# Four-head decoder layer on one Trainium2 core: the third head's scores and value products as split float32r products, like the last head's

## The chip, the core and the metric

The kernel runs on one core of a Trainium2 chip. The metric is the time of one launch on the device in microseconds (us); lower is better. The engines in the text are TensorE (PE in the profile, its weight loads PEld), VectorE (DVE), ScalarE (ACT), GpSimd (POOL) and the queues that issue transfers: SP's own and ACT's (ACTq), which issues them in the order of ACT's instructions.

## The reference

One layer over 512 positions of width 1024: conditioned RMS norm, one input projection, four matrix-memory heads (mLSTM) of width 256 beside a gated convolution group, an output projection, and a gated feed-forward part with a short convolution. All is float32. The part that matters here is a head. The reference does it by chunks:

```python
scores = jnp.einsum("bhtd,bhsd->bhts", q_, k_) * jnp.exp(dmat - m_t[..., None])
num = (w_inter[..., None] * jnp.einsum("bhtd,bhde->bhte", q_, C)
       + jnp.einsum("bhts,bhse->bhte", scores, v_))
den = w_inter * jnp.einsum("bhtd,bhd->bht", q_, n) + jnp.sum(scores, axis=-1)
h = num / jnp.maximum(jnp.abs(den), jnp.exp(-m_t))[..., None]
```

The kernel has no chunks with a carried state: it forms the whole causal 512 x 512 matrix of weighted scores of a head, in four block rows of keys, and multiplies it by the values with a column of ones, which gives numerator and denominator together.

## The kernel before

**Two kinds of product.** A float32 matmul is issued to PE as two instructions. For nearly all large products the kernel does something else: it splits each operand into a rounded part hi (float32r, made by an ACT copy) and the rest lo (source less hi, made by a subtraction on DVE or POOL), and adds up hi·hi, hi·lo and lo·hi as three float32r matmuls (`mm3`, lines 186 to 190). `w_split` (164) splits weights with ACT and POOL, `pair` (451) splits an activation with ACT and DVE.

**The heads.** For head h, `head_load` (475) brings the weights of q, k and the output gate as three pieces of 1 MB (`wqko`), and `head_proj(h, i)` (481) makes the six projections of 128 x 512: i = 0, 1 for q, 2, 3 for k, 4, 5 for the gate `so`. A q or k goes through `conv4` (456): one ACT instruction at line 460, three taps on DVE at line 462, a silu on ACT at 463. `make_v(h)` (416) makes the values in four blocks, `make_E(h)` (598) the four block rows of decay factors E.

**attention(h)** (500) is a generator, so that its pieces can be put between the projections of the next head. First come the scores, one PSUM tile `s` per block row cc (keys cc·128 on, 512, 384, 256 and 128 columns), two at a time; DVE multiplies each into E (line 515). Then the products with the values, one tile `o` for each block tt of positions (1, 2, 3 and 4 block products, ten in all); ACT reads each `o` (lines 536 to 538). After that DVE scales (549), PE transposes into two tiles `hT` (555), and DVE and ACT make the head's result in two parts (557 to 561).

**Which head is split.** `SPLIT = (H - 1,)` (412) names the heads whose scores and value products are done by three float32r products instead of float32 matmuls. In the kernel before that is head 3 alone.

**Order.** PE and SP run in the order of the code. DVE, ACT and POOL get theirs from a scheduler at build time, which puts the 31-tap convolution (`cv_block`, 714, line 731 on DVE) and the conditioning sums (`ada_block`, 147: a load on the ACT queue into one of two buffers, then a product with a sum on DVE at line 155, tile `junk`) behind all else. Every engine then runs its list strictly in order. In the loop at 782, with h = 2, PE does: scores 0 and 1 of head 2, projection 0 of head 3, scores 2 and 3, projections 1 and 2, `o` 0 and 1, projection 3, `o` 2, projection 4, `o` 3, projection 5, then the values of head 3 with the two `hT` in between.

**Buffers.** PSUM is shared out as four banks for projections and values (`mmbank`, 87) and two (`atbank`, 90) that `s`, `o`, `hT` and a few others take in turn: a new one can begin when the tile two before it has been read. In SBUF there are 44 slots of 128 x 512 for q, k, E, their parts and the rest.

Of the kernel before, what the change touches and what calls it, by code (L numbers as in the profile page):

```python
# [22 lines left out]
H = 4  # L23
# [29 lines left out]
def decoder_layer(ctx, tc, w_glu0, x, xT, c, adaT, vecs, w_glu, w_qko, w_v0, w_v, w_out, w_up, w_down, out):  # L53
# [30 lines left out]
    def slot(name, dt=F32):  # L84
        return slots.tile([P, T], dt, tag="t", name=name)
# [78 lines left out]
    def w_split(src, name, pool=None, tag="w", eng=None):  # L164

        n = src.shape[1]
        pool = pool or wpool
        hi = pool.tile([P, T], F32R, tag=tag, name=f"{name}h")
        lo = pool.tile([P, T], F32R, tag=tag, name=f"{name}l")
        S.activation(hi[:, :n], src, AF.Copy)  # L170
        (eng or G).tensor_tensor(out=lo[:, :n], in0=src, in1=hi[:, :n].bitcast(F32), op=ALU.subtract)  # L171
        return hi, lo
# [236 lines left out]


    vs = [None] * H
    SPLIT = (H - 1,)
    gz = const.tile([P, NT, 2 * H], F32, name="gz")
    GB = 2 * H

    def make_v(h):
# [3 lines left out]
        for q in range(0, KT, 4):  # L420
# [6 lines left out]
            else:  # L427
                wv += [tuple(w[:, :n] for w in w_split(r[:, i * n : (i + 1) * n], f"wv{h}_{q + i}")) for i in range(4)]
        dt = F32R if h in SPLIT else F32
        va = vpool.tile([P, 2 * T + 8], dt, tag="vh", name=f"v{h}").rearrange("p (c n) -> p c n", c=NT)  # L430

        V.tensor_copy(va[:, :, DH:], ones[:, None, :2].to_broadcast([P, NT, 2]))
        vs[h] = [va[:, cc, :] for cc in range(NT)]
        if h in SPLIT:
            vl = [slot(f"vl{h}_{i}", F32R) for i in range(2)]
# [3 lines left out]
        for tt, ps in enumerate(banks):  # L439
# [5 lines left out]
            S.activation(va[:, tt, :DH], ps[:, :DH], AF.Copy)  # L445
            if h in SPLIT:
                V.tensor_tensor(out=vl[tt], in0=ps[:, :DH], in1=va[:, tt, :DH].bitcast(F32), op=ALU.subtract)
# [52 lines left out]
    def attention(h):  # L500

        _, qs, ks, so = heads[h]
        two = h in SPLIT
        if two:
# [277 lines left out]
    for h in range(H - 1):  # L782
# [14 lines left out]
        next(steps)  # L797
        if h + 1 in SPLIT:
            for zs in heads[h + 1][1:3]:
# [538 lines left out]
```

## Time and profile before

| | |
|---|---|
| median of 3 runs | 771.67 us (771.31 to 774.28) |
| the profiled execution: its time, its span | 773.07 us, 771.4 us |
| granted TensorE clock, mean | 0.997 |
| busy in the span: PE, DVE, ACT, POOL | 758.4, 610.1, 403.8, 352.2 us |
| scores of head 2 in the span | 261.3 to 264.5 and 269.9 to 272.0 us |
| value products of head 2 | in three groups from 282.9, 289.6 and 296.4 us |
| scores of head 3 | 317.9 to 320.4 and 323.2 to 324.5 us |

How to read the profile: a row of the timeline gives the start in us from the begin of the span, the duration of the row, engine, line, operation, tile written and tiles read, shapes, the count of merged instructions, and in brackets the idle time of the engine just before with what released it. Matmuls are pipelined, so a row's duration overlaps the next row; what a matmul costs PE is the distance from its start to the next start. DVE rows overlap the next by some 0.08 us in the same way.

### The profile page before, as it was taken

The numbers are of one execution on the slowest core, as the hardware profiler recorded it, in microseconds if no ns is written. First come the engines' busy times: TensorE is split into PE (matmuls) and PEld (weight loads), VectorE is DVE, ScalarE is ACT, GpSimd is POOL, SyncE is SP. The second block draws the span as 40 slices with busy tenths as digits, with TensorE's granted clock in tenths as the row PEclk, the third lists the DMA queues.
The fourth block names the chain that finished last, engine by engine and source line by source line (L and its number), as shares of the span: only waits on it lengthen the run. The fifth ranks groups of instructions, "written<-read, shape, count | busy, mean of one in ns | idle before, by whom it ended". The sixth has DMA issues, their size and how long they took to land.

```text
span 771.4 us, 10631 instructions
## 1 busy us (share of the span) xinstructions
PE 758.4 (98%) x3709; PEld 637.5 (83%) x3709; DVE 610.1 (79%) x967; ACT 403.8 (52%) x761; POOL 352.2 (46%) x286
## 2 busy tenths in 40 slices
PE   7999999999999999999999999999999999999996
PEld 5788898778888888988888998888888888888885
DVE  6997999999999966756768798666556687799995
ACT  5447266776666447582253555444444444455762
POOL 2029578696798645443661456444444440000001
PEclk9999999999999999999999999999999999999998
DMA  8983214214022452434953753332233321777872
GB/s 320 377 301 132 90 55 164 82 40 151 30 84 107 153 179 105 164 110 164 366 199 126 253 197 130 130 130 88 110 117 129 130 89 62 255 271 241 298 260 109
DMA packets 36409, 125.33 MB, mean 162 GB/s; under 512 B 4194, under 2 KB 5634, under 8 KB 30468
## 3 DMA queue, kind: packets, MB, share of 16 engines
q1 hardware_dynamic: 24372, 96.17, 35.5%
q10 hardware_dynamic: 11984, 28.48, 10.6%
q8 instruction: 29, 0.48, 0.3%
q14 instruction: 24, 0.20, 0.1%
HBM read 113.22 MB, written 11.42 MB: 162 GB/s over the span
## 4 chain that ended last, share of the span: by engine, by line
PE 72%; DVE 21%; DMA 2%; ACT 2%; issue 2%; POOL 0%; ACTq 0%; DVEq 0%; POOLq 0%
PE up L189 10%; PE up L188 10%; DVE cv L731 10%; PE up L190 10%; PE p L1185 4%; PE glu L189 3%; PE glu L190 3%; PE glu L188 3%; PE p L189 3%; PE p L188 3%; PE p L190 3%; PE mixa L188 2%; PE mixa L190 2%; PE mixa L189 2%; PE mixb L189 2%; PE mixb L188 2%
## 5 line engine op out<-in xcount | busy, mean ns | idle before, releaser
L731 DVE SCALAR_TENSOR_TENSOR cv<-gt,cvw,cv 128x505 f32<-128x505 f32 (+24 forms) x200 | 137.3, 729 | 2.3 <-ACT cv L719 1.1
L685 POOL TENSOR_TENSOR ro2r<-ro2t,mhalf 128x1 f32<-128x1 f32 x1 | 0.5, 537 | 119.8 <-DVE ro2t L683 119.8
L727 POOL TENSOR_TENSOR cs<-cs,cs 128x510 f32<-128x510 f32 (+3 forms) x32 | 41.9, 1308 | 0.3
L171 POOL TENSOR_TENSOR wup_1024l<-wup,wup_1024h 128x512 fp32r<-128x512 f32 x20 | 27.4, 1372 | 31.6 <-ACT wup_1024h L170 31.6
L171 POOL TENSOR_TENSOR wup_0l<-wup,wup_0h 128x512 fp32r<-128x512 f32 x20 | 27.7, 1387 | 30.0 <-ACT wup_0h L170 30.0
L171 POOL TENSOR_TENSOR wup_1536l<-wup,wup_1536h 128x512 fp32r<-128x512 f32 x20 | 28.0, 1399 | 27.6 <-ACT wup_1536h L170 25.1
L155 DVE SCALAR_TENSOR_TENSOR junk<-ada,cb 128x1024 bf16<-128x1024 f32 x20 | 31.3, 1565 | 8.5 <-DMA ada<-in_adaT 8.4
L189 PE MATMUL up<-u2l,wup_0h 128*128 128x512 f32 (+1 forms) x100 | 36.5, 365 | 0.2 <-DVE u2l L910 0.2
L188 PE MATMUL up<-u2h,wup_0h 128*128 128x512 f32 (+1 forms) x100 | 36.5, 365 | 0.0
L188 PE MATMUL up<-u2h,wup_1024h 128*128 128x512 f32 (+1 forms) x100 | 36.4, 364 | 0.0
L190 PE MATMUL up<-u2h,wup_0l 128*128 128x512 f32 (+1 forms) x100 | 36.4, 364 | 0.0
L188 PE MATMUL up<-u2h,wup_512h 128*128 128x512 f32 (+1 forms) x100 | 36.4, 364 | 0.0
L189 PE MATMUL up<-u2l,wup_512h 128*128 128x512 f32 (+1 forms) x100 | 36.4, 364 | 0.0
L190 PE MATMUL up<-u2h,wup_512l 128*128 128x512 f32 (+1 forms) x100 | 36.4, 364 | 0.0
L188 PE MATMUL up<-u2h,wup_1536h 128*128 128x512 f32 (+1 forms) x100 | 36.4, 364 | 0.0
L189 PE MATMUL up<-u2l,wup_1536h 128*128 128x512 f32 (+1 forms) x100 | 36.4, 364 | 0.0
L190 PE MATMUL up<-u2h,wup_1536l 128*128 128x512 f32 (+1 forms) x100 | 36.4, 364 | 0.0
L190 PE MATMUL up<-u2h,wup_1024l 128*128 128x512 f32 (+1 forms) x100 | 36.4, 364 | 0.0
L189 PE MATMUL up<-u2l,wup_1024h 128*128 128x512 f32 (+1 forms) x100 | 36.3, 363 | 0.0
L171 POOL TENSOR_TENSOR wup_512l<-wup,wup_512h 128x512 fp32r<-128x512 f32 x20 | 27.7, 1383 | 14.0 <-ACT wup_512h L170 14.0
L725 ACT ACTIVATE cs<-gt,cvw 128x511 f32<-128x511 f32 (+4 forms) x40 | 27.4, 716 | 6.5 <-POOL cs L727 3.2
L170 ACT ACTIVATE wup_1024h<-wup 128x512 fp32r<-128x512 f32 x22 | 13.9, 631 | 25.1 <-PE up L189 20.4
(1072 smaller groups left out, 2667.0 us busy)
## 6 DMA issues: line engine op xcount, KB each, us to landing
wup<-in_w_up SPq DMA_DIRECT2D x22, 1024.0 KB, 6.5
wqko<-in_w_qko SPq DMA_DIRECT2D x12, 1024.0 KB, 4.8
ada<-in_adaT ACTq DMA_DIRECT2D x20, 512.0 KB, 4.6
ada<-in_adaT SPq DMA_DIRECT2D x16, 512.0 KB, 6.9
wo<-in_w_out SPq DMA_DIRECT2D x8, 1024.0 KB, 4.8
spare<-in_adaT ACTq DMA_DIRECT2D x12, 512.0 KB, 7.4
wd<-in_w_down SPq DMA_DIRECT2D x6, 768.0 KB, 6.7
g2kept<-g2d SPq DMA_DIRECT2D x11, 384.0 KB, 7.3
```

The lines of the kernel that those rows point to most:

```text
L155: t = V.scalar_tensor_tensor(out=junk, in0=r, scalar=1.0, in1=cb, op0=ALU.mult, op1=ALU.mult, accum_out=mod[:, i : i + 1])
L170: S.activation(hi[:, :n], src, AF.Copy)
L171: (eng or G).tensor_tensor(out=lo[:, :n], in0=src, in1=hi[:, :n].bitcast(F32), op=ALU.subtract)
L188: PE.matmul(ps, a[0], b[0], start=start, stop=False)
L189: PE.matmul(ps, a[0], b[1], start=False, stop=False)
L190: PE.matmul(ps, a[1], b[0], start=False, stop=stop)
L685: G.tensor_tensor(out=r, in0=t, in1=mhalf[:, :1], op=ALU.pow)
L725: S.activation(t[:, d:], cvx[j][:, : T - d], AF.Copy, scale=w(CK - 1 - d))
L727: G.tensor_tensor(out=side[:, d:], in0=side[:, d:], in1=t[:, d:], op=ALU.add)
L731: last_tap[0] = V.scalar_tensor_tensor(out=cp[:, d:], in0=cvx[j][:, : T - d], scalar=w(CK - 1 - d), in1=cp[:, d:], op0=ALU.mult, op1=ALU.add)
L1185: PE.matmul(ps[q], x, y, start=False, stop=m == NM - 1 and i == 2, skip_group_check=True)
```

## The change

Head 2 joins the heads that are split:

```diff
-    SPLIT = (H - 1,)
+    SPLIT = (H - 2, H - 1)
```

This one line selects branches that are there already. In `make_v(2)` the values are stored as a float32r part, still by one ACT copy per block, and line 447 adds a subtraction on DVE for the rest (`vl`), which reads the PSUM bank of the block too. In the loop, after projection 4 of head 2, its two q and two k tiles are split by `pair`. In `attention(2)`:

```python
if two:
    mm3(sp[:, :n], [z[:, cc * P : (cc + 1) * P] for z in ks[d]], [z[:, cc * P :] for z in qs[d]], d == 0, d == 1)
else:
    PE.matmul(sp[:, :n], ks[d][:, cc * P : (cc + 1) * P], qs[d][:, cc * P :], start=d == 0, stop=d == 1)
...
if two:
    E[h][cc] = pair(E[h][cc], *halves_e[cc])
...
    PE.matmul(o[:, : DH + 2], eh, vh, start=cc == 0, stop=False)
    PE.matmul(o[:, :DH], eh, vl, start=False, stop=False)
    PE.matmul(o[:, : DH + 2], el, vh, start=False, stop=cc == tt)
else:
    PE.matmul(o[:, : DH + 2], E[h][cc][:, a : a + P], vs[h][cc], start=cc == 0, stop=cc == tt)
```

So PE has 3 instructions for every 2 in head 2's scores and value products. DVE gets 12 instructions more: four `qkl`, four `vl`, four `El`. ACT gets 8 more: four `qkh`, four `Eh`. No transfer is added, and outside head 2 nothing is computed in another way. The order on DVE and ACT is made anew.

On DVE, the four `qkl` of head 2 come between the taps of the last convolution block (tile `cv`, columns 492 downward); `dm` belongs to head 1:

```order
 L731 SCALAR_TENSOR_TENSOR cv_2298<-gt_912,cvw,cv_2298 128x492
+L453 TENSOR_TENSOR qkl_2480<-q_0c,qkh_2479 128x512
 L731 SCALAR_TENSOR_TENSOR cv_2298<-gt_912,cvw,cv_2298 128x491
-L432 CAST v_3021<-ones 128x4x2
+L432 CAST v_3093<-ones 128x4x2
+L453 TENSOR_TENSOR qkl_2484<-q_1c,qkh_2483 128x512
 L543 TENSOR_TENSOR dm_2379<-dm_2379,em 128x4
 L731 SCALAR_TENSOR_TENSOR cv_2298<-gt_912,cvw,cv_2298 128x490
+L453 TENSOR_TENSOR qkl_2488<-k_2c,qkh_2487 128x512
+L453 TENSOR_TENSOR qkl_2492<-k_3c,qkh_2491 128x512
 L731 SCALAR_TENSOR_TENSOR cv_2298<-gt_912,cvw,cv_2298 128x489
```

All that follows on DVE (the rest of the taps, then the conditioning sums and the E of head 2) stands behind them; the four `vl` are put in one by one further down, the last of them just ahead of the first E.

On DVE, from the first E of head 2 to the taps of head 3's first q (`q_0c`). Before:

```order
L515 SCALAR_TENSOR_TENSOR E_2510<-s_0_2720,E_2510 128x512
L155 SCALAR_TENSOR_TENSOR junk_3180,mod<-ada_3178,cb 128x1024
L515 SCALAR_TENSOR_TENSOR E_2511<-s_1_2724,E_2511 128x384
L155 SCALAR_TENSOR_TENSOR junk_3184,mod<-ada_3182,cb 128x1024
L155 SCALAR_TENSOR_TENSOR junk_3188,mod<-ada_3186,cb 128x1024
L160 TENSOR_TENSOR mod<-mod,vec 128x8
L667 SCALAR_TENSOR_TENSOR gains<-mod,vec 128x8
L515 SCALAR_TENSOR_TENSOR E_2512<-s_2_2759,E_2512 128x256
L462 SCALAR_TENSOR_TENSOR q_0c<-qko_0_2728,vec,q_0c 128x511
L515 SCALAR_TENSOR_TENSOR E_2511<-s_3_2763,E_2511 128x128
L462 SCALAR_TENSOR_TENSOR q_0c<-qko_0_2728,vec,q_0c 128x510
L462 SCALAR_TENSOR_TENSOR q_0c<-qko_0_2728,vec,q_0c 128x509
```

And with the change, from the third row of that stretch (E 0 and E 1 now stand together just ahead of it) to the second tap:

```order
L155 SCALAR_TENSOR_TENSOR junk_3248,mod<-ada_3246,cb 128x1024
L453 TENSOR_TENSOR El_2745<-E_2526,Eh_2742 128x512
L155 SCALAR_TENSOR_TENSOR junk_3252,mod<-ada_3250,cb 128x1024
L453 TENSOR_TENSOR El_2746<-E_2527,Eh_2743 128x384
L515 SCALAR_TENSOR_TENSOR E_2528<-s_2_2799,E_2528 128x256
L155 SCALAR_TENSOR_TENSOR junk_3256,mod<-ada_3254,cb 128x1024
L515 SCALAR_TENSOR_TENSOR E_2527<-s_3_2809,E_2527 128x128
L462 SCALAR_TENSOR_TENSOR q_0c<-qko_0_2768,vec,q_0c 128x511
L453 TENSOR_TENSOR El_2747<-E_2528,Eh_2744 128x256
L155 SCALAR_TENSOR_TENSOR junk_3260,mod<-ada_3258,cb 128x1024
L453 TENSOR_TENSOR El_2746<-E_2527,Eh_2743 128x128
L462 SCALAR_TENSOR_TENSOR q_0c<-qko_0_2768,vec,q_0c 128x510
```

Four conditioning sums now stand between E 1 and the taps of `q_0c` where there were two, and four `El` with them.

On ACT, from the weights of head 3's values to the reading of the first `o` of head 2 (`dm`, `hn`). Before:

```order
L463 ACT_TABLE_LOAD
L463 ACTIVATE q_0c<-q_0c 128x512
L170 ACTIVATE wv_1h<-wv_0_3001 128x512
L460 ACTIVATE q_1c<-qko_1_2767,vec 128x512
L170 ACTIVATE wv_4h<-wv_4_3011 128x512
L463 ACTIVATE q_1c<-q_1c 128x512
L170 ACTIVATE wv_5h<-wv_4_3011 128x512
L460 ACTIVATE k_2c<-qko_2_2798,vec 128x512
L536 ACTIVATE dm_2830<-o_0_2833 128x1
L537 ACTIVATE hn_0_2831<-o_0_2833 128x256
```

With the change:

```order
L170 ACTIVATE wv_1h<-wv_0_3073 128x512
L463 ACT_TABLE_LOAD
L463 ACTIVATE q_0c<-q_0c 128x512
L460 ACTIVATE q_1c<-qko_1_2819,vec 128x512
L170 ACTIVATE wv_4h<-wv_4_3083 128x512
L463 ACTIVATE q_1c<-q_1c 128x512
L170 ACTIVATE wv_5h<-wv_4_3083 128x512
L460 ACTIVATE k_2c<-qko_2_2850,vec 128x512
L536 ACTIVATE dm_2882<-o_0_2885 128x1
L537 ACTIVATE hn_0_2883<-o_0_2885 128x256
```

One weight copy (`wv_1h`) has moved ahead of the table load; the reading of `o` 0 stands behind the same two silus and the same two first steps of `conv4` as before.

## The prediction

> **What bounds the kernel now.** I read the page's first part, then busy time by stretch around head 2, then the timeline of PE, DVE and ACT there.
>
> ```profile
> span 771.4 us, 10631 instructions
> PE 758.4 (98%) x3709; PEld 637.5 (83%) x3709; DVE 610.1 (79%) x967; ACT 403.8 (52%) x761; POOL 352.2 (46%) x286
> ...
> core 0: us, PE busy (x) PEld busy (x) DVE busy (x) ACT busy (x) POOL busy (x), PEclk, DMA share, GB/s
> 236.00:261.00 25.00, 25.00 (x160) 22.65 (x158) 23.04 (x35) 11.96 (x29) 15.33 (x14) 1.00 0.27 85
> 261.00:281.00 20.00, 19.23 (x81) 14.76 (x81) 16.62 (x23) 7.37 (x12) 12.87 (x7) 1.00 0.62 207
> 281.00:304.00 23.00, 23.00 (x103) 19.14 (x103) 11.60 (x18) 15.01 (x38) 12.33 (x11) 1.00 0.40 140
> ```
>
> PE is the bound: 98% of the span, and in the three stretches around head 2 it idles 0.77 us in all, at full clock. So PE time saved there is saved at the end, and a wait of PE there is paid in full. DVE is not far behind: 23 of 25 us before 261, 16.6 of 20 after it. What the change adds to DVE lands in just these stretches; the question is whether PE ever comes to need something that DVE or ACT now makes later.
>
> **What PE saves.** The scores of head 2 before, and those of head 3, which have the form that head 2 will get:
>
> ```profile
> 261.34 1.12 PE L514 MATMUL s<-q_0c,k_2c 128*128 128x512 f32 x2 [0.33 <-DVE so L557]
> 262.30 1.02 PE L514 MATMUL s<-q_1c,k_3c 128*128 128x512 f32 x2
> 263.16 0.81 PE L514 MATMUL s<-q_0c,k_2c 128*128 128x384 f32 x2
> 264.68 0.39 PE L189 MATMUL qko<-ul,wqko_0h 128*128 128x512 f32 x1
> 264.91 0.40 PE L190 MATMUL qko<-uh,wqko_0l 128*128 128x512 f32 x1
> ...
> 269.93 0.59 PE L514 MATMUL s<-q_0c,k_2c 128*128 128x256 f32 x2
> 271.40 0.49 PE L514 MATMUL s<-q_0c,k_2c 128*128 128x128 f32 x2 [0.45 <-DVE E L515]
> 272.18 0.39 PE L189 MATMUL qko<-ul,wqko_1024h 128*128 128x512 f32 x1
> ...
> 317.88 0.48 PE L188 MATMUL s<-qkh,qkh 128*128 128x512 f32 x1
> 320.40 0.39 PE L188 MATMUL mixa<-wo_0h,hh 128*128 128x512 f32 x1
> 323.17 0.28 PE L188 MATMUL s<-qkh,qkh 128*128 128x256 f32 x1
> 323.88 0.22 PE L188 MATMUL s<-qkh,qkh 128*128 128x128 f32 x1
> 324.50 0.55 PE L203 MATMUL ry_b<-ident,ry_r 128*128 128x128 f32 x3
> ```
>
> A 512-column product matmul costs 0.23 us (264.68 to 264.91), so the first group of head 2 ended at 264.68 - 0.23 = 264.45: 3.11 us. The second ended at 271.95: 2.02 us, with a wait in it. Together 5.13. Head 3 takes 320.40 - 317.88 = 2.52 and 324.50 - 323.17 = 1.33, together 3.85. So up to 1.28 us come off, of which about 0.8 are waits and starts that the new form need not lose: two float32 instructions at 512 columns take 0.86 (262.30 to 263.16), which scaled to all block rows (2 x 1280/512 x 0.86) makes 4.30, and 4.30 - 3.85 = 0.45 is the pure saving.
>
> The value products:
>
> ```profile
> 283.02 1.31 PE o L533 x6
> 289.62 1.47 PE L533 MATMUL o<-v,E 128*128 128x258 f32 x6
> 336.33 0.28 PE L529 MATMUL o<-v,Eh 128*128 128x258 f32 x1
> 336.45 0.28 PE L530 MATMUL o<-vl,Eh 128*128 128x256 f32 x1
> ```
>
> Six float32 instructions took 1.31 us (first row, from the chain of waits), 0.218 each; a split one takes 0.12. Ten block products: 20 x 0.218 = 4.36 against 30 x 0.12 = 3.60, a saving of 0.76 (0.23 in `o` 0 and 1, 0.53 in the rest). PE's total: 1.2 us pure, 2.0 us if every wait goes, and with the idle 0.33 ahead of the first score 2.4 at the very most, 0.3% of the time.
>
> **What DVE and ACT get, and when it is late.** Head 3's own split gives the durations:
>
> ```profile
> L453 DVE TENSOR_TENSOR El<-E,Eh x4: 279/616/1636, 321.1 to 325.4; 128x512 fp32r<-128x512 f32 x1, 128x384 fp32r<-128x384 f32 x1, 128x256 fp32r<-128x256 f32 x1, 128x128 fp32r<-128x128 f32 x1
> L453 DVE TENSOR_TENSOR qkl<-q_1c,qkh x1: 678/678/678, 298.9 to 298.9; 128x512 fp32r<-128x512 f32 x1
> L447 DVE TENSOR_TENSOR vl<-v,v x4: 409/412/418, 310.9 to 317.9; 128x256 fp32r<-128x256 f32 x4
> L155 DVE SCALAR_TENSOR_TENSOR junk<-ada,cb 128x1024 bf16<-128x1024 f32 x8 | 14.1, 1766 | 3.7 <-DMA ada<-in_adaT 3.6
> ```
>
> Four `qkl`, the first at 0.87 (at 298.09 in a row below) and three near 0.68, make 2.95 us, four `vl` 1.65, four `El` 0.81 + 1.64 + 0.42 + 0.28 = 3.15: 7.75 us more for DVE, less 0.08 of overlap each, so 6.8. ACT's eight more copies (0.62 each at 512 columns) fill idle time, for ACT is busy 7.4 of 20 us in the stretch from 261.
>
> First place: the scores. Score 2 needs the bank that E 0 reads, score 3 that of E 1.
>
> ```profile
> 252.89 1.22 DVE L155 SCALAR_TENSOR_TENSOR junk<-ada,cb 128x1024 bf16<-128x1024 f32 x1
> 258.54 2.13 DVE L155 SCALAR_TENSOR_TENSOR junk<-ada,cb 128x1024 bf16<-128x1024 f32 x1 [1.57 <-DMA ada<-in_adaT]
> 261.80 1.21 DVE L155 SCALAR_TENSOR_TENSOR junk<-ada,cb 128x1024 bf16<-128x1024 f32 x1
> 268.56 0.68 DVE L515 SCALAR_TENSOR_TENSOR E<-s,E 128x512 f32<-128x512 f32 x1
> ```
>
> Four `qkl` and one `vl` ahead of the first `junk` move it from 252.9 to about 256.2. But in the new order only two `junk` stand ahead of the `so` step, not three, and the wait of 1.57 us for a load is gone. With two `junk` (1.2 and 2.2), a `vl`, the 0.68 of `ydl`, and `so`, `vl`, `so` (0.6, 0.4, 0.6), DVE is at 262.2, against 261.80 before. So PE's scores begin within 0.3 us of where they did, say 261.1. Then `junk`, `hl`, `junk`, `hl` take 6.76 us as before (261.80 to 268.56), the last `vl` 0.4: E 0 is done at about 269.9, E 1 at 270.5. PE ends scores 0 and 1 at 261.1 + 2.5 = 263.6, projection 0 at 263.6 + 24 x 0.227 = 269.1, waits 0.8 for E 0, and ends score 3 at 271.2, against 271.95 before. So far 0.8 us gained: the waits before are not so much removed as exchanged.
>
> Second place: `o` 2, which needs the bank of `o` 0, free once ACT has run `hn` of `o` 0. That stands on ACT behind q_0c's silu, which waits for q_0c's last tap on DVE.
>
> ```profile
> 278.28 1.52 DVE L462 SCALAR_TENSOR_TENSOR q_0c<-qko,vec,q_0c 128x510 f32<-128x510 f32 x2
> 279.88 1.28 ACT L463 ACT_TABLE_LOAD   x1 [1.98 <-DVE q_0c L462]
> 281.71 0.62 ACT L170 ACTIVATE wv_1h<-wv 128x512 fp32r<-128x512 f32 x1
> 282.23 0.76 ACT L460 ACTIVATE q_1c<-qko,vec 128x512 f32<-128x512 f32 x1
> 287.21 0.38 ACT L537 ACTIVATE hn<-o 128x256 f32<-128x256 f32 x1
> ```
>
> The last tap ended at 279.80 and `hn` at 287.59: 7.8 us of ACT and DVE in turn (table load, silus, the taps of q_1c). The new order takes `wv_1h` out of that chain, 0.52 us, so 7.3. `o` 2 began at 289.62: a slack of 2.0 us. Now the taps: from E 1 (270.5) DVE has four `junk` (4 x 1.77), four `El` (3.15), two E (0.71) and three taps (2.24), 13.2 us, less 1.0 of overlap: they end at 282.7, 2.9 late. `hn` of `o` 0 is done at 290.0. PE without a wait would reach `o` 2 at 289.62 - 0.8 - 0.23 = 288.6. It waits 1.4 us. Of the gain of 1.03 nothing is left there, and 0.53 come with the rest of `o`: the sum is -1.03 + 1.4 - 0.53 = -0.2 us.
>
> Bounds of this wait. If POOL disturbs nothing (`junk` at 1.21, `El` scaled from 0.68, in all 2.0), DVE's sum would end near 279.4. But the loads set a floor: with two buffers, a load goes out when the `junk` two before has read its buffer, and it is there some 4.4 us later:
>
> ```profile
> 254.15 4.30 DMA ada<-in_adaT
> ```
>
> The first of the four ends at 271.7, so the third starts at 276.1 at the earliest, and with what stands behind it (two `junk`, an E, two `El`, three taps, 5.6 us with the overlap off) the taps end at 281.7 at best. The wait is then 0.4 at most. If all `junk` take the longest 2.31 and every `El` twice its time, they end near 287 and it is 5.3.
>
> The lateness then dies out. ACT and DVE have gaps behind this place, and the next needs of PE are far off:
>
> ```profile
> 292.02 2.32 DVE L462 SCALAR_TENSOR_TENSOR k_3c<-qko,vec,k_3c 128x511 f32<-128x511 f32 x3 [2.40 <-ACT k_3c L460]
> 298.09 0.87 DVE L453 TENSOR_TENSOR qkl<-q_0c,qkh 128x512 fp32r<-128x512 f32 x1 [3.75 <-ACT qkh L452]
> ```
>
> Head 3's split begins after DVE idled 3.75 us, and its parts are used by PE at 317.88; if that cover were gone, each us late would cost one. The banks of head 2's values, which the `vl` now hold longer, are wanted by head 3's projections, the last `vl` (269.2) by projection 3 at 283: 14 us of cover.
>
> [...]
>
> ```profile
> 321.30 1.74 POOL L171 TENSOR_TENSOR wo_512l<-wo,wo_512h 128x512 fp32r<-128x512 f32 x1
> ```
>
> `El` 1 took 1636 ns where its 384 columns need about 0.5 by the 678 ns of a `qkl`, while POOL ran a weight split. [...]
>
> **The rivals, and how the numbers follow.** The sum is made against the profiled span of 771.4 us; that execution took 773.07 us, and the median of the runs is 771.67. I put the change on the median.
>
> *Forecast, 0.48:* PE's gain is mostly eaten by the wait at `o` 2: -0.2 us, 771.4. Its own range, from no wait at `o` 2 (-1.6) to 1.5 us more of it, is 770.1 to 773.2.
>
> *Everything hides, 0.12:* the new order removes both old waits and makes none, -2.0 to -2.4 us: 769.5. For it speaks that the loads no longer hold up DVE; against it that E 0 must follow one `vl` and the same four instructions.
>
> *Slower, 0.30:* DVE against POOL. If the four `qkl` and four `El` each lose about 1 us (as `El` 1 did), E 0 comes 4 us later, score 2 waits 4 us more, and the taps end 8 us later, at 290.7; `hn` is done at 298.0, `o` 2 starts 8.4 us later than before, and with the 0.53 the end is 8 us late. Half of that, 4 us, gives 775.7. It decides from the point where the last tap of q_0c ends after 286.7: at 282.8 gain and wait cancel, and 3.9 us more are 0.5%.
>
> *The change doesn't do what it says, 0.03:* the split form costs PE as much as float32. At 128 columns it may (head 3's score 3 takes 324.50 - 323.88 = 0.62 us, float32 at that width 271.95 - 271.40 = 0.55), but not at 512. `o` 2 would still start at 290.0, set by ACT, 0.4 later than before, and nothing comes back behind it: 772.1.
>
> *Faster by a gain that I can't place, 0.07:* more than 3.9 us cannot come from PE's products, which give 2.4 at most; it would need stretches outside head 2, where the order is the same.
>
> A difference under 0.5%, 3.9 us, can't be told from no change here. Faster by more: 0.07. Slower by more: about four fifths of the slower case, 0.24. The rest, 0.69, is within. The range for 8 in 10 runs from 768.8, below the full gain, up to 776.2, a little past the 775.7 of the slower case.
>
> **What would show it.** Right: PE's scores of head 2 in 2.5 and 1.3 us without waits, its `o` at 0.12 per matmul; a PE wait of about 0.8 for E 0 ahead of score 2; the last tap of q_0c at 282 to 283; a PE wait of 1 to 2 us ahead of `o` 2, released by ACT; nothing changed after 304 but a common shift. Wrong: a last tap before 281 (then the second case), DVE rows of `qkl` and `El` well over 1 us and score 2 later than 272 (then the third), or a PE wait at head 3's scores, which I take to be covered.

## The result, and the profile after

| | before | with the change |
|---|---|---|
| median, runs taken side by side | 772.7 us (771.31 to 775.01, 15 runs) | 774.88 us (773.56 to 777.73, 15 runs) |
| ratio, 95% interval | | 1.0032 [1.0022, 1.0042] |
| profiled execution: time, span | 773.07, 771.4 us | 776.73, 775.0 us |

The kernel became 0.3% slower, about 2.2 us, where 0.2 us of gain was forecast. The time lies inside the range, and within 0.5%, but on the other side of zero.

The page of the changed kernel, first part:

```profile
span 775.0 us, 10690 instructions
PE 759.2 (98%) x3727; PEld 639.2 (82%) x3727; DVE 617.3 (80%) x979; ACT 407.9 (53%) x769; POOL 354.7 (46%) x286
```

DVE has 7.2 us more than the 610.1 of before, where 6.8 were foretold. Busy time by stretch (length, then PE, PEld, DVE, ACT, POOL), the same three stretches as in the prediction:

```profile
236.00:261.00 25.00, 25.00 (x155) 22.61 (x154) 24.33 (x39) 14.99 (x35) 15.47 (x14) 1.00 0.11 44
261.00:281.00 20.00, 17.85 (x92) 14.97 (x91) 20.00 (x26) 7.69 (x15) 13.53 (x9) 1.00 0.58 186
281.00:304.00 23.00, 21.40 (x109) 17.98 (x108) 12.80 (x22) 15.51 (x38) 11.05 (x10) 1.00 0.46 161
```

From 261 to 281 DVE is busy all of the 20.00 us (16.62 before), and PE idles 2.15 us there and 1.60 in the next stretch. PE's waits by what released them (total, times, longest):

```profile
PE o L529 <- ACT hn L537: 1.6, 1, 1.6
PE s L188 <- DVE E L515: 1.5, 1, 1.5
...
PE s L188 <- DVE so L557: 0.7, 1, 0.7
```

These three are new or grown; before there were 0.33 us for `so` and 0.45 for E (the rows at 261.34 and 271.40 in the prediction), and none for `hn`.

How much is that in sum? The two executions differ already when they reach head 2, so I measure from a row of each execution's own: from the last group of values of head 2 to `Mb`, which opens the part behind head 2. In the timeline of PE, before:

```profile
257.90 0.36 PE L188 MATMUL v<-wv_0h,uh 128*128 128x256 f32 x1
...
303.62 0.39 PE L600 MATMUL Mb<-Ms,rowsel 128*128 128x512 f32 x1
```

and with the change, with the three waits in between:

```profile
259.62 0.36 PE L188 MATMUL v<-wv_0h,uh 128*128 128x256 f32 x1
...
263.41 0.50 PE L188 MATMUL s<-qkh,qkh 128*128 128x512 f32 x1 [0.68 <-DVE so L557]
...
273.07 0.39 PE L188 MATMUL s<-qkh,qkh 128*128 128x256 f32 x1 [1.47 <-DVE E L515]
...
293.75 0.39 PE L529 MATMUL o<-v,Eh 128*128 128x258 f32 x1 [1.60 <-ACT hn L537]
...
307.27 0.39 PE L600 MATMUL Mb<-Ms,rowsel 128*128 128x512 f32 x1
```

45.72 us before, 47.65 after: 1.93 us lost between these rows, and the distance behind them is the same to the end of the program within 0.03 us. The 1.72 us by which the changed kernel is already late at 257.90 arise in the first 39 us, where nothing was changed; in twelve further profiles below this row lies between 256.80 and 259.32, so that is scatter of single executions. The loss in the medians, 2.2 us, agrees with 1.93. I call the distance between the two rows the stretch; and "on the clock of before" means 1.72 us subtracted.

DVE, with the change:

```profile
249.68 3.21 DVE L549 TENSOR_SCALAR hn<-hn,fac 128x256 f32<-128x256 f32 x4 [0.28 <-POOL fac L546]
...
263.61 0.67 DVE L557 SCALAR_TENSOR_TENSOR so<-so,hT 128x512 f32<-128x512 f32 x1
264.20 2.25 DVE L155 SCALAR_TENSOR_TENSOR junk<-ada,cb 128x1024 bf16<-128x1024 f32 x1
...
272.01 0.41 DVE L447 TENSOR_TENSOR vl<-v,v 128x256 fp32r<-128x256 f32 x1
272.34 1.14 DVE L515 SCALAR_TENSOR_TENSOR E<-s,E 128x512 f32<-128x512 f32 x2
...
274.55 1.77 DVE L453 TENSOR_TENSOR El<-E,Eh 128x512 fp32r<-128x512 f32 x1
276.24 2.31 DVE L155 SCALAR_TENSOR_TENSOR junk<-ada,cb 128x1024 bf16<-128x1024 f32 x1
...
283.55 1.22 DVE L155 SCALAR_TENSOR_TENSOR junk<-ada,cb 128x1024 bf16<-128x1024 f32 x1 [1.85 <-DMA ada<-in_adaT]
...
285.68 0.75 DVE L462 SCALAR_TENSOR_TENSOR q_0c<-qko,vec,q_0c 128x509 f32<-128x509 f32 x1
```

E 0 and E 1 are done at 273.48 - 1.72 = 271.8 on the clock of before (270.5 foretold for E 1), and the last tap of `q_0c` at 286.43 - 1.72 = 284.7 (282.7 foretold). Both places were named; DVE comes to both of them later than forecast.

### The profile page after: what moved, and what is told of

Read it like the earlier page. It is cut to its first block, busy times and chain, and to the rows that moved or that the text cites. A ratio compares the mean times of both kernels' runs of the same rounds, so it can differ in the third digit from the quotient of the medians.

```text
span 775.0 us, 10690 instructions
## 1 busy us (share of the span) xinstructions
PE 759.2 (98%) x3727; PEld 639.2 (82%) x3727; DVE 617.3 (80%) x979; ACT 407.9 (53%) x769; POOL 354.7 (46%) x286
## 4 chain that ended last, share of the span: by engine, by line
PE 69%; DVE 21%; ACT 3%; DMA 3%; issue 2%; POOL 1%; ACTq 0%; SPq 0%; DVEq 0%; POOLq 0%
PE up L189 10%; PE up L190 10%; PE up L188 10%; DVE cv L731 10%; PE p L1185 4%; PE glu L189 3%; PE glu L190 3%; PE glu L188 3%; PE p L190 3%; PE p L189 3%; PE p L188 3%; PE mixa L190 2%; PE mixa L188 2%; PE mixa L189 2%; PE mixb L188 2%
```

## The experiments

**Theory.** PE's own saving is there, and DVE is late at E and at the taps because of all that stands on it in order, above all the eight conditioning sums. **Rivals.** The saving isn't real; the two PSUM banks for `s` and `o` bind by themselves; the loads of the sums, on ACT's queue, hold ACT up.

In the table, "stretch" is the distance from the last value group to `Mb` less the 45.72 us of before, and "behind" the change of the distance from `Mb` to the product `mixa` at 325.36 (21.74 us before), both from the timeline of PE. Both are of one execution each, the profiled one. The +5.87 and the +5.59 each hold some 3 us that a halved TensorE clock cost (see the last section).

| run | ratio to before, interval | stretch | behind |
|---|---|---|---|
| the change | 1.0032 [1.0022, 1.0042] | +1.93 | 0.0 |
| scores alone | 0.9988 [0.9978, 0.9998] | -0.88 | 0.0 |
| values alone | 0.9965 [0.9952, 0.9978] | -1.82 | 0.0 |
| change, more banks | 1.0011 [0.9992, 1.0029] | -1.66 | +5.87; again +2.85 |
| change, sums among head 3's taps | 1.0006 [0.9992, 1.0019] | -2.60 | +2.44 |
| the same, loads by SyncE | 1.0048 [1.0033, 1.0064] | -2.61 | +5.16 |
| the same, loads by GpSimd | 1.0014 [1.0000, 1.0028] | -2.61 | +5.59 |
| change, sums last | 1.0287 [1.0260, 1.0315] | -2.60 | 0.0 |
| before, sums last | 1.0307 [1.0283, 1.0331] | -1.27 | 0.0 |
| values alone, sums last | 1.0305 [1.0279, 1.0332] | -2.07 | 0.0 |
| change, sums in two halves | 1.0000 [0.9982, 1.0018] | -2.60 | 0.0 |
| before, sums in two halves | 1.0015 [0.9998, 1.0032] | -1.27 | 0.0 |

**Each half of the change alone.** First only the scores of head 2 (its q and k split, E and values as before):

```diff
-        if h + 1 in SPLIT:
+        if h + 1 in (H - 2, H - 1):
...
-                if two:
+                if h >= H - 2:
                     mm3(sp[:, :n], ...)
```

(to the kernel before), then only its value products (E and values split, q and k not):

```diff
-        if h + 1 in SPLIT:
+        if h + 1 == H - 1:
...
-                if two:
+                if h == H - 1:
                     mm3(sp[:, :n], ...)
```

(to the changed kernel).

> Of the change only the scores of head 2: its q and k are split and its scores are three float32r products; its E, its values and the value products stay float32 as before. DVE gets the four qkl and none of the vl and El. Theory (PE's saving is paid back in two waits for PSUM banks that DVE's lateness sets): score 2 still waits some 0.8 us for E 0, the scores come out about 0.7 us shorter than before, o 2 waits about 1 us for ACT; sum +0.3 us, ratio to before 1.0004. Rival (the loss of the change comes from the split products themselves or from outside head 2): the scores carry their share of it, ratio 1.0015 or more with no PE wait at o 2.

> Of the change only the value products of head 2: its values and E are split, its q and k and its scores stay float32 as before. DVE gets the four vl and four El and none of the qkl. Theory: the E come 1.4 us later than before by the four vl, score 2 or 3 waits for them, the last tap of q_0c ends near 281.5 and o 2 waits little or not; with the 0.76 us of the products the sum is -0.4 us, ratio 0.9995. Rival (the loss comes from the products or from outside): ratio 1.0015 or more.

772.53 and 770.89 us against 773.36: 0.8 and 2.5 us faster, while both together are 2.2 slower. Both gained more than expected, and the waits that were expected ahead of score 2 and `o` 2 came in neither. The halves do not add up: -3.3 against +2.2 in the medians, -2.70 against +1.93 in the stretch. So some 5 us are lost when they come together; that they meet on DVE is the theory, which the runs below test. PE's own saving is not shown by these two runs yet, for a new order on DVE that removes waits would make them faster too. With the values alone DVE has just the `vl` and `El`, and E 0 and E 1 now stand together; the row on DVE:

```profile
267.69 1.14 DVE L515 SCALAR_TENSOR_TENSOR E<-s,E 128x512 f32<-128x512 f32 x2
```

Before, a sum of 1.71 us stood between the two (E 0 at 268.56, E 1 at 270.80). PE then waits for neither `so` nor E, and the whole stretch gains 1.82 us: 0.80 of it from `o` 0 on, from the products, and 1.02 ahead of that, where the two waits were. The other 0.7 us of the median I can't place.

**More banks.** `s` 2 and 3 and `o` 2 and 3 of head 2 in the two banks of the convolution, which are free by then. It takes the wait for E 0 and for `hn` away and leaves the order on DVE and ACT as it was:

```diff
-            sp = atbank(f"s{h}_{cc}")
+            sp = (cvbank if h == H - 2 and cc >= 2 else atbank)(f"s{h}_{cc}")
...
-            o = atbank(f"o{h}_{tt}")
+            o = (cvbank if h == H - 2 and tt >= 2 else atbank)(f"o{h}_{tt}")
```

> The change whole, with the two PSUM banks of the convolution, idle by then, for scores 2 and 3 and for o 2 and o 3 of head 2. The order on DVE and ACT is the same. Theory: both waits of PE (1.5 us for E 0, 1.6 us for ACT's hn) vanish and nothing takes their place; -3.1 us against the change, -1.2 against before, ratio 0.9985. Rival (the loss lies outside head 2, as in the 1.7 us that the profiled execution of the change lost in its first 16 us, ahead of all that was changed): the ratio stays near 1.003. Second rival (the lateness only moves on to the next bank, that of a projection): half of the gain, ratio 1.0005 to 1.002, with a new PE wait at a qko or v row.

> A second profile of the run with the conv's two banks for scores and products 2 and 3 of the third head; its first profile was of an execution 4 us above its median. If VectorE's lateness is what TensorE meets after 304 once the banks let it run ahead, the waits ahead of ry_s and s (1.6 and 0.9 us) are there again within 0.5 us; if they belong to that one execution they are below 0.8 together and the time is below 773.

774.01 us, 1.0011. The stretch gains 1.66 us, more than the 1.2 expected, and all of it and more is lost behind: the second rival's wait came, in another place. PE's waits there, in the first profile:

```profile
PE ry_s L196 <- DVE so L557: 1.6, 1, 1.6
...
PE s L188 <- DVE ry_t L209: 0.9, 1, 0.9
```

and in the second:

```profile
PE ry_s L196 <- DVE so L557: 1.2, 1, 1.2
PE s L188 <- DVE ry_t L209: 1.1, 1, 1.1
```

So they belong to the kernel. From `hn` to the last `hl` DVE runs with one gap of 0.34 us (305.8 to 320.7 in the first profile); where PE no longer waits at E and `o` 2, it meets a late DVE there. It is even later than in the changed kernel, for it stands longer in front of the eighth sum. In DVE's timeline of the first profile:

```profile
283.81 1.23 DVE L155 SCALAR_TENSOR_TENSOR junk<-ada,cb 128x1024 bf16<-128x1024 f32 x1 [3.69 <-DMA ada<-in_adaT]
```

That is 3.69 us (3.09 in the second profile), against 1.85 in the changed kernel: from the issue of its load to its start 6.8 us pass here, 5.0 there. Why the load takes longer was not tried.

**The sums among head 3's taps.** Sums 16 to 23 held behind the last tap of `q_0c`:

```diff
         head_proj(h + 1, 1 if h == 0 else 0)
+        q0_tap = last_conv4[0]
...
-        ada_block(i, last_tap[0])
+        ada_block(i, q0_tap)
```

> The change whole, with the eight conditioning sums (junk, line 155) held back until the last tap of head 3's q_0c; they then stand between the taps of q_1c, k_2c and k_3c. Theory: E 0 is done 4 us earlier, score 2 waits for nothing, the scores save their 1.3 us and the 0.3 ahead of them; the taps of q_0c end near 277 and the first wait is gone, but the sums and their loads now stretch the taps of q_1c, and o 2 may wait up to 1.5 us; -0.6 to -2.1 us against before, ratio 0.997 to 0.999. Rival (the loss is not DVE's lateness): ratio near 1.003.

773.55 us, 1.0006, short of the expectation, though the mechanism in it held: all three waits are gone and the stretch is 2.60 us shorter. 2.44 us go behind, to waits ahead of `ry_s` (0.75) and `s` (1.11) again and what hangs on them. The sums now stand between the taps of k, and ACT stands behind their loads, which must wait until a sum frees a buffer. In ACT's timeline of this run:

```profile
285.29 0.78 ACT L460 ACTIVATE k_2c<-qko,vec 128x512 f32<-128x512 f32 x1 [2.87 <-DVE junk L155]
...
292.87 0.78 ACT L460 ACTIVATE k_3c<-qko,vec 128x512 f32<-128x512 f32 x1 [2.76 <-DVE junk L155]
```

Was it ACT's queue, then? The same with the loads of sums 18 to 23 on another queue (`nc.sync`, then `nc.gpsimd`):

```diff
-        nc.scalar.dma_start(r, adaT[i // 2]...)
+        (nc.sync if 18 <= i < 24 else nc.scalar).dma_start(r, adaT[i // 2]...)
```

> As the run with the sums behind the last q tap of the last head, with the loads of sums 18 to 23 issued by SyncE instead of ScalarE. There the stretch from 258 to 304 was 2.6 us shorter than before and the next one gave 2.45 back, as ScalarE stood 2.9, 2.8 and 2.1 us behind such loads, so that k_2c, k_3c and the last qkh rows, and with them hn, came late. Theory (ScalarE's queue behind the loads is what took the gain back): the waits ahead of ry_s (0.8) and s (1.1) are gone or below 0.3, ratio 0.997 to 0.998. Rival (VectorE itself is full there, whoever issues the loads): both waits stay, ratio 1.000 to 1.001. Second rival (loads that leave only at 278, behind those of the last head's value weights, hold VectorE's taps up): new waits of TensorE at o 2, o 3 or hT, ratio 1.002 or more.

> The same with the loads of sums 18 to 23 issued by GpSimd, between its splits of the value weights. Theory: as with SyncE, 0.997 to 0.998. Rival (GpSimd's splits wv_1l to wo_0l now stand behind the loads, and the values' product waits for them): a wait of TensorE ahead of v at 304 of 1 us or more, ratio 1.001 or more.

776.65 and 774.27 us: the theory on ACT's queue fell, for the two waits stay (1.60 and 1.10 with SyncE, 1.61 and 0.63 with GpSimd). It is not excluded that the queue has a part, as the loads of sums 24 and 25 stayed on it. GpSimd's own rival, a wait ahead of `v` at 304, did not come. With GpSimd issuing, DVE itself sits in front of sums whose load isn't there, with k's taps behind them:

```profile
281.35 1.23 DVE L155 SCALAR_TENSOR_TENSOR junk<-ada,cb 128x1024 bf16<-128x1024 f32 x1 [2.33 <-DMA ada<-in_adaT]
...
291.66 1.22 DVE L155 SCALAR_TENSOR_TENSOR junk<-ada,cb 128x1024 bf16<-128x1024 f32 x1 [1.83 <-DMA ada<-in_adaT]
...
295.57 1.81 DVE L155 SCALAR_TENSOR_TENSOR junk<-ada,cb 128x1024 bf16<-128x1024 f32 x1 [1.23 <-DMA ada<-in_adaT]
```

Eight sums over two buffers took 25 us here (273.8 to 299.2), 22.7 with SyncE (274.0 to 296.8), 26 in the changed kernel (258.7 to 284.8) and 24 before (252.9 to 276.8): whoever issues the loads, the sums stay spread over more than 22 us, though each takes 1.2 to 2.3. The run with SyncE waits 1.65 us at `hT` besides, as its second rival said.

One more thing makes DVE late in these three runs and in both profiles with more banks: the four `hn` of head 2 lie beside two splits of GpSimd there. In DVE's timeline of the first of the three:

```profile
304.38 3.21 DVE L549 TENSOR_SCALAR hn<-hn,fac 128x256 f32<-128x256 f32 x4 [0.91 <-POOL fac L546]
```

They take 3.2 us in all five profiles, and 2.17 beside one split in the kernels before and after. That is 1 us of DVE's time on the way to `so`, for which `ry_s` waits. (The run with the scores alone has 3.18 there too, but no wait: its PE is only 0.88 us early.)

**The sums last.** All eight and their gain behind the last head's `hl`, and the transpose of the gain (`gT`) behind the first output product; then the same in the kernel before, and with the values alone:

```diff
-    for i in range(16, 24):
-        ada_block(i, last_tap[0])
-    ada_done(16, 24)
-    gain(0, 16, "mix_post_g")
...
+    for i in range(16, 24):
+        ada_block(i, last_lo[0])
+    ada_done(16, 24)
+    gain(0, 16, "mix_post_g")
     for i in range(24, 40):
         ada_block(i, last_lo[0])
...
     for n in range(10, 2 * KT):
         mix_first(n)
-        if n == 10:
-            send_rows(0, KT)
+    send_rows(0, KT)
```

> The change with the eight sums 16 to 23 (L155, about 14 us of VectorE between 250 and 285) and the gain that follows them put behind the last head's hl rows, and the transpose of that gain put behind the whole first output product. Theory (VectorE is late at both places because of its whole load there, and ScalarE behind the loads of these sums): the waits of TensorE for E (1.5), hn (1.6) and so (0.7) are gone, as are the 0.3 and 0.4 that the kernel before has; TensorE's own 1.2 us show, so the stretch from 258 to 304 is 1.5 to 2.4 us shorter than before and the ratio is 0.997 to 0.998, if nothing new waits where the sums go. Rival (the two banks for scores and products bind by themselves, not VectorE): the waits at E and hn stay within 0.5 us of 1.5 and 1.6 and the ratio is 1.002 or more. Second rival (the next stage, 304 to 321, where VectorE runs hn to hl without a gap, takes the gain back, as in the run with the sums behind the last q tap): the stretch to 304 is 1.5 to 2.4 shorter and a wait of 0.7 or more stands ahead of ry_s or s, ratio 0.999 to 1.001.

> The kernel before with the same eight sums moved to the same place. Theory: it has only 0.3 us (so) and 0.4 us (E) of waits of TensorE to lose between 258 and 304, so 0.999 to 0.9995. Rival (the sums cost something else that this move takes away or adds, such as a load on ScalarE's queue): outside 0.998 to 1.0005.

> Only the value products of the third head in three parts (E and values split, scores float32) and the eight sums moved to the same place. The run with the values alone was 0.9965 and has no wait of TensorE between 258 and 304 left, so by the theory the sums have nothing to give: 0.996 to 0.997. Rival (sums cost TensorE something even where no wait is shown): 0.9955 or less; second rival (a new wait where the sums go): 0.998 or more.

794.93, 796.34 and 795.84 us: the ratios of all three expectations missed by 3%, because the sums do not fit where I put them. The stretch missed too: 2.60 where 1.5 to 2.4 were expected, 1.27 where 0.7 were, and 2.07 where nothing beyond the 1.82 of the run with the values alone was. PE's two longest waits of the first of them:

```profile
PE gT L653 <- ACT wup_0h L170: 10.2, 1, 10.2
PE gT L653 <- DVE gains L667: 9.7, 1, 9.7
```

For head 2 they are the cleanest runs all the same, since that cost comes after it. With the change, in PE's timeline:

```profile
257.64 0.36 PE L188 MATMUL v<-wv_0h,uh 128*128 128x256 f32 x1
...
300.76 0.39 PE L600 MATMUL Mb<-Ms,rowsel 128*128 128x512 f32 x1
```

without it:

```profile
256.80 0.36 PE L188 MATMUL v<-wv_0h,uh 128*128 128x256 f32 x1
...
301.25 0.39 PE L600 MATMUL Mb<-Ms,rowsel 128*128 128x512 f32 x1
```

43.12 against 44.45 us, and no wait between the rows in either. So without the sums the change is worth 1.33 us of PE time: 0.80 for the value products (44.45 against the 43.65 of the run with the values alone) and 0.53 for the scores. The medians of the two runs differ by 1.4 us as well. What the kernel before loses there to its two waits is 1.27, of which its profile shows 0.78 as idle time. Nothing waits ahead of `ry_s` and `s` either: the split by itself does not make DVE late there. The rival of the two banks falls with it, for here they are as before.

**The sums in two halves.** 16 to 19 behind the last tap of `q_0c`, 20 to 23 and the gain behind the last `yl`, where DVE had gaps; `gT` stays:

```diff
-    for i in range(16, 24):
-        ada_block(i, last_tap[0])
-    ada_done(16, 24)
-    gain(0, 16, "mix_post_g")
+    for i in range(16, 20):
+        ada_block(i, q0_tap)
...
     mix_first(4)
+    for i in range(20, 24):
+        ada_block(i, last_tap[0])
+    ada_done(16, 24)
+    gain(0, 16, "mix_post_g")
```

(with `q0_tap` as above and `last_tap` set at the `yl` rows; then the same in the kernel before).

> The change with the eight sums split: 16 to 19 behind the last head's last q_0c tap, among the taps, 20 to 23 and the gain behind the last yl row, where VectorE stood idle from 340.9 to 354.2 in the kernel before; the transpose of the gain stays where it was. Theory (the whole cost of the change is VectorE's rows in order ahead of E and of the taps; with the sums out of the way TensorE loses nothing): TensorE is 2.6 us earlier than before at 304 against its own value rows at 258, as in all runs with the sums taken out, and nothing waits ahead of ry_s, s or gT for more than 0.3 us, so 0.996 to 0.9975, faster than the values alone or level with them. Rival (four sums among the taps are still too many, as the eight were): 1 us or more of waits ahead of ry_s and s, ratio 0.998 to 1.000. Second rival (sums 20 to 23 make hn, hl or the gain of the last head late): a wait ahead of hT at 353 or gT at 357, ratio 0.9985 or more.

> The kernel before with the sums split in the same way. Theory: 1.3 us earlier at 304, as with all its sums last, and nothing taken back: 0.998 to 0.999, so that the change itself, with the sums out of its way, is worth 1.3 us or 0.0017. Rival (the change is worth nothing or less even so): level with or below the run beside it.

772.83 and 774.97 us, both short of the expectation. The first rival did not come, for nothing waits ahead of `ry_s` and `s`. The stretch is again -2.60 and -1.27, and nothing is lost up to 357. But 1.6 and 2.4 us are lost at the second `gT`, at 392.7; in the run with the change:

```profile
PE gT L653 <- DVE gains L868: 1.4, 1, 1.4
```

Sums 24 to 39 feed that `gT`. Their last row on DVE in the kernel before:

```profile
390.84 1.23 DVE L863 TENSOR_SCALAR gains<-gains 128x8 f32<-128x8 f32 x1
```

and here:

```profile
389.88 1.20 DVE L868 TENSOR_SCALAR gains<-gains 128x8 f32<-128x8 f32 x1
```

It ended at 392.07 before, just ahead of `gT` at 392.71. Here it ends at 391.08; this execution was 0.45 us early at 257.90, so on the clock of before that is 391.5. The sums are 0.5 us earlier, PE 2.6, the kernel before had 0.5 us to spare there, and the rest is waited off. (In the run without the change the trace puts the wait, 2.2 us, down to ACT's `mixa3junk`, which ends at 395.07 together with DVE's `gains`; both chains start from the last sum.) Once more most of the saving ends at the next thing that hangs on the sums. 1.03 us of it are left at `gT` in this profile; why the median shows nothing of them is in the last section. Between the two of this pair the change is worth 2.1 us (772.83 against 774.97, with intervals that overlap): 1.33 in the stretch and 0.8 at the second `gT`. With the sums where they were it is -2.2: by where eight sums stand, the same edit loses or gains. The best version in the study is the one with the values alone, 0.9965 [0.9952, 0.9978].

## Why the prediction was wrong

**What PE saves: right.** 1.2 us pure were forecast, 1.33 measured: 0.80 in the value products (forecast 0.76) and 0.53 in the scores (0.45). The most that could go, 2.4 us, was set a little low: 2.60, since the waits and starts of the kernel before were worth 1.27, where 0.8 and 0.33 had been counted.

**The two places: right.** PE waits at score 2 for E 0 and at `o` 2 for ACT's `hn`, and nowhere behind. (The wait for `so` ahead of score 0 grew as well, from 0.33 to 0.68 us; the scores were to begin at 261.1 and began at 263.41 - 1.72 = 261.7.) The `hn` of `o` 0 in ACT's timeline:

```profile
293.32 0.38 ACT L537 ACTIVATE hn<-o 128x256 f32<-128x256 f32 x1
```

From the last tap to its end ACT took 293.70 - 286.43 = 7.27 us, forecast 7.3. The wait at `o` 2 was 1.60 us, forecast 1.4. From the last tap on the path was right altogether: gain and wait were to cancel with a last tap at 282.8; it came at 284.7, 1.9 later, and 1.93 us were lost.

**The step that failed: DVE's time up to E 0.** The prediction had "`junk`, `hl`, `junk`, `hl` take 6.76 us as before". They took 264.20 to 272.01, 7.81 us. The second `so` ended nearly where it was forecast, 264.28 - 1.72 = 262.6 against 262.2; then the first `junk` of the four took 2.25 us, not the 1.21 of before. This single duration was carried over unchanged to a row that had moved against POOL's rows. POOL, with the change:

```profile
249.62 1.30 POOL L171 TENSOR_TENSOR wqko_0l<-wqko,wqko_0h 128x512 fp32r<-128x512 f32 x1
250.87 1.33 POOL L171 TENSOR_TENSOR wqko_512l<-wqko,wqko_512h 128x512 fp32r<-128x512 f32 x1
...
264.07 1.30 POOL L171 TENSOR_TENSOR wqko_1024l<-wqko,wqko_1024h 128x512 fp32r<-128x512 f32 x1
```

and before:

```profile
246.22 1.44 POOL L171 TENSOR_TENSOR wqko_0l<-wqko,wqko_0h 128x512 fp32r<-128x512 f32 x1 [0.73 <-ACT wqko_0h L170]
...
261.80 2.35 POOL L171 TENSOR_TENSOR wqko_1024l<-wqko,wqko_1024h 128x512 fp32r<-128x512 f32 x1 [2.21 <-ACT wqko_1024h L170]
```

The split of `wqko_1024l` and this `junk` meet in both kernels. Before, they start together at 261.80, the `junk` takes 1.21 us and the split 2.35; with the change the split is 0.13 us ahead, it takes 1.30 and the `junk` 2.25. The fourteen traces of this case hold 448 such sums: the 225 that began while GpSimd had nothing running took 1.20 to 1.23 us, and of the 223 others 200 took more than 1.3, up to 2.32. Near meetings elsewhere in the kernel before went the same way: the sum at 271.97 began 0.08 us ahead of a split and took 1.22 us, the split 2.30; the sum at 274.66 began 0.27 us behind a split and took 2.11 us, the split 1.30. In these the one that came first kept its time. The `hn` at 249.68 is another such row. Its four instructions lie beside two splits and take 3.21 us; before, beside one split, they took 2.17:

```profile
245.90 2.17 DVE L549 TENSOR_SCALAR hn<-hn,fac 128x256 f32<-128x256 f32 x4
```

The prediction looked for this contention, but ahead of E 0 only in the instructions that the change adds, and gave it a case of its own at 8 us. Of these the `qkl` (0.87 us and three of 0.68) and the `vl` (0.41 to 0.42) lost nothing, and the four `El` took 3.02 us where 3.15 were taken; the instructions that were there already lost 1.04 (`hn`) and 1.04 (`junk`). At the second `so` only 0.4 us of the loss at `hn` show. That was luck: the sum up to there had counted its rows without their overlap, and the second `junk` took 1.99 us where 2.2 were taken. The other 1.0 of the 1.3 us at E 0 and E 1 is the `junk`. No run here moved GpSimd's splits, so the cause of these two longer rows is read from the traces and not tried.

**The second term that was mis-sized: the floor of the loads.** It was worked out for the buffer of the first of the four sums. The eighth sum uses the other one, which the sixth freed at 278.55; its load was there at 283.55, and DVE stood 1.85 us in front of it. From E 1 to the last tap DVE took 284.7 - 271.8 = 12.9 us, forecast 12.2. It is only 0.7 more by luck, since the four sums took 5.95 us there and not the 7.08 of the forecast.

Put together: E 1.3 us later and the taps another 0.7 make 2.0 us at the last tap; `o` 2 starts at 292.03 on the clock of before, forecast 290.0; the sum is +1.93, forecast -0.2. (Two slips of addition in the prediction change nothing of this: 771.67 - 0.2 is 771.5, and 1.5 us more of the wait make 773.0, not 773.2.)

**The cover behind: right for this kernel, wrong as a cover in itself.** Head 3's split did not delay PE, but because PE was late. In the runs of the whole change where PE came 1.66 or 2.6 us earlier and all eight sums still stood ahead of head 3's split, PE waited 1.9 to 2.7 us at `ry_s` and `s`; where four of them or none did, it waited for nothing there.

## What to carry to other kernels

Where PE is busy 98% and another engine 80%, an edit that moves work from PE to that engine is worth what the second engine's order allows: list what stands on it ahead of each row that PE waits for, and expect the saving to come back at the next row that is late once the first wait is gone. Don't carry a duration over to a place where the row will stand beside other rows of GpSimd, also not that of an instruction which the edit leaves alone: here the same sum took 1.2 or 2.3 us. Try the halves of an edit apart: here each half gains, the values alone 0.35%, and both together lose.

## What the runs showed of the hardware

In the profiles of two runs a wait of PE of 1.6 us was followed by a halved clock, which cost more than the wait. In the first profile of the run with more banks, after the wait of 1.60 us ahead of `ry_s`, the granted clock (behind the five engines' busy times) fell to half:

```profile
316.00:319.00 3.00, 1.51 (x11) 1.42 (x12) 3.00 (x7) 1.53 (x3) 0.21 (x1) 1.00 0.00 0
...
321.00:326.00 5.00, 4.81 (x13) 4.26 (x14) 3.17 (x6) 1.30 (x3) 4.81 (x4) 0.50 0.93 324
```

PE's timeline of the same execution:

```profile
323.70 0.63 PE L189 MATMUL mixa<-wo_0l,hh 128*128 128x512 f32 x1
324.13 0.63 PE L190 MATMUL mixa<-wo_0h,hl 128*128 128x512 f32 x1
...
326.60 0.39 PE L190 MATMUL mixa<-wo_0h,hl 128*128 128x512 f32 x1
326.83 0.40 PE L188 MATMUL mixa<-wo_0h,hh 128*128 128x512 f32 x1
```

Matmuls of 512 columns start 0.43 us apart, and 0.23 again from 326.60 on. That is why "behind" is +5.87 in this profile and +2.85 in the second of the same kernel, which has nearly the same waits and a mean clock of 0.999, where the first has 0.994: some 3 us for the clock alone. The profile of the run with GpSimd's loads shows the same after a wait of 1.61 us ahead of `ry_s`: matmuls of 512 columns start 0.43 us apart between 319 and 325 and 0.23 from 325.51 on, with a mean clock of 0.994. In that run six of twelve executions had a mean clock of 0.993 to 0.995 and took 776.0 us in the mean, the six others, at 0.997 to 0.999, 773.2. In the run with the change and the sums in two halves, four of twelve had 0.993 to 0.996 and took 774.6 us in the mean, the eight others 771.9; the kernel before, run beside it, had 0.997 or more in all 23 executions and took 772.9. So the 1 us that its profile, at 0.999, has left shows only in the executions with the higher clock. The three waits of the changed kernel itself, 0.68 to 1.60 us, were not followed by it in the profiled execution, whose clock is 1.00 in all three stretches from 236 to 304. The waits ahead of the two halved stretches were 1.60 and 1.61 us, each with eight one-column products (1.05 us) behind it. The run with SyncE, with waits of 1.65 us at `hT` and 1.60 at `ry_s`, had a mean clock of 0.998 in its profile. What decides whether an execution is hit was not tried.
